# A two-block sequence model on one core: S5's Toeplitz matrices written out whole, one sum per rotation, and a later place for the GLU's splits

## The chip, the core and the metric

The kernel runs on one core of one Trainium2 chip. The metric is the device time of one execution in microseconds, lower is better. Engines are called TensorE (PE in the rows; PEld are its weight loads), VectorE (DVE), ScalarE (ACT), GpSimd (POOL) and SyncE (SP); SP issues every DMA of this program.

## The reference

A model of 256 tokens and 1024 features, all float32. Block one has two layers, each a mixer and a feed-forward with squared ReLU of width 4096, both modulated by a condition vector; the mixer of layer 0 is a gated convolution beside retention, that of layer 1 is S5. A second block follows: gated linear attention, forgetting attention, attention into a memory, gates, and a SwiGLU. The part that the change touches is S5: 64 groups of 16 channels each drive 64 complex states, forward and backward in time,

```
h_t = a h_(t-1) + B u_t          (complex, diagonal a, one system per direction)
y   = Re(C_f h_f) + Re(C_b h_b) + D u
out = (gelu(y) W_a) * sigmoid(gelu(y) W_b)
```

## The kernel before

Activations lie as [128 features, 8 blocks, 256 tokens]. Every dense product runs in three passes of TensorE on weights split in two float32r parts: `piece` (line 309) loads 1 MB of weights by a DMA on SP into one of four buffers (`load`, line 296), and `hilo` (lines 313 to 315) makes of it the high part on ScalarE and the low part on VectorE, a quarter at a time; `lin` (line 323) multiplies. The modulation weights (`ada`, line 429) go through the same four buffers.

**The order of instructions.** The code is traced in order, and a planner then orders each engine's instructions by a simulated time line: on each engine the earliest traced of those that are ready comes first. What is traced as `paced` (line 938) is pinned on TensorE, VectorE and ScalarE behind what was traced last there; SP is not pinned. Each engine then runs its list strictly in order. A tile pool of n buffers makes the writer of a buffer wait for the last reader of the tile that had it.

**S5.** The 256 steps are cut into 32 chunks of 8. Inside a chunk the output is a product with Toeplitz matrices of the kernels at lags -7 to 7; between chunks the states are carried by a scan. All matrices depend on parameters alone. `s5_tables` (line 884) makes them for four groups at a time (i = 0 to 15), a step at a time between the pieces of layer 0's mixer and feed-forward: the matrix from states to outputs V and its write to DRAM (line 897), the kernels by matrix products into one PSUM bank (line 907), their copy by ScalarE into the staging tile Ks, which holds four i and has one buffer (line 911), the matrix from inputs to states W (lines 920 to 922), its transposes by TensorE into the same PSUM bank (line 928), ScalarE's copies (line 929) and their write (line 932). After i = 3, 7, 11 and 15 the four kernels in Ks go to DRAM, each lag once, as rows of 15 lags (lines 916 and 917): eight DMAs.

Layer 1's `s5` (line 956) turns the input into U and Ur by TensorE, then does eight steps (ip), each with two i. `load` (line 1010) reads the tables of a step two steps ahead: W and V in two DMAs each (line 1001), for each pair of steps the Toeplitz matrices Mt by eight DMAs that read overlapping runs of 128 numbers out of the rows of lags (line 1019), and it makes dm, the decay factors of the scan, on GpSimd and ScalarE (lines 1023 and 1024). `chunk_states` makes what each chunk adds to the state (lines 1037 to 1043). `scan` (line 1050) does on VectorE: two products with cosine and sine (1056, 1057), a sum and a difference into PSUM (1058, 1059), the scan (1060), two products back (1064, 1065); then four sums and differences on GpSimd (1067, 1068). `outputs` (line 1071) multiplies by Mt (1079) and V (1081), and for each two steps ScalarE copies the result to Y (1114). `finish` (line 1083) transposes Y, adds D u (1094), applies GELU (1095) and splits the result, for the first half of the steps' channels and at the end for the second. The GLU follows with four pairs of weight pieces; the splits of the first pair are held on VectorE behind the last step's scan:

```
            S = scan(pT.pop(ip), tabs[ip])
            scanned = {mybir.EngineType.DVE: self.last(mybir.EngineType.DVE)}
...
            if j == 0:
                with self.held_at(scanned):
                    Wa, Wb = self.piece("glu_a", j), self.piece("glu_b", j)
```

Of the kernel before, what the change touches and what calls it, by code (L numbers as in the profile page):

```python
# [14 lines left out]
T = 256  # L15
EPS = 1e-6

# columns of the packed per-feature vectors
# [11 lines left out]
def layout(v):  # L30
    """Rearranges the inputs for the DMA engines; no value is changed."""
# [20 lines left out]
    # the same weights with a column to a partition  # L52
# [20 lines left out]
    # S5: group g = 16 e + i, stored in the order (i, e); d = direction  # L73
# [41 lines left out]
class Fill:  # L115
    """Work that is traced a step at a time between the steps of something else."""
# [16 lines left out]
    def settle(self):  # L133
        """Traces the generator that has begun to its end."""
        if self.gens and self.begun is self.gens[0]:
            self.drain(len(self.gens) - 1)

    def drain(self, left=0):
        """Traces all but the last `left` of the generators to their end."""
        while len(self.gens) > left:  # L140
            for _ in self.gens.pop(0):
                pass
        self.credit = 0.0


class Sums:
    """Sums over the features of x^2 w by token, two feature blocks at a time; w(c) [128, m] for block c."""
# [11 lines left out]
    def total(self):  # L159
        """Adds up the squares at hand: one call behind them, so that TensorE need not wait."""  # L160
# [14 lines left out]
class K:  # L175
    def __init__(self, tc, I, out, dbg):
# [4 lines left out]
        self.ntab = {"Wt": 1, "Vt": 1, "Mt": 2, "dm": 2}  # L181
# [37 lines left out]
    def later(self, by):  # L219
        """What is traced here gives way to everything up to `by` instructions further on."""  # L220
# [11 lines left out]
    def last(self, engine):  # L232
        """The name of the last instruction traced on engine."""
        return next(i for i in reversed(list(self.nc.cur_bb.bb.instructions)) if i.engine == engine).name

    def after(self, fill, n, engine, anchor):
        """n steps of fill; on the engine they are issued after the anchor."""
# [8 lines left out]
    def held(self, *engines):  # L246
        """What is traced here is issued behind what was traced last on the engines."""
# [12 lines left out]
    def pinned(self, fill):  # L260
        """The rest of fill, on some engines behind what was traced last."""
# [9 lines left out]
    def behind(self, fill, n=None):  # L271
        """Steps of fill, on DVE behind what was traced last."""
# [10 lines left out]
    # ---- storage  # L283
# [11 lines left out]
    # ---- weights: DMA, split into two float32r parts  # L295
# [27 lines left out]
    def lin(self, ps, W, act, ks, start=True, stop=True, cols=(0, 1)):  # L323
        """ps [128, len(cols), 256] += W[:, k, col block]^T act[:, k']; ks pairs (k of W, k of act)."""
# [6 lines left out]
    def lin_tok(self, ps, W, act):  # L331
        """ps [128 tokens, 2 halves, 256 columns] = act^T W."""
# [24 lines left out]
    def sumsq(self, x, st=None):  # L357
        """[128 tokens, 2 halves, m]: the sums over the features of x^2 w, x [128, 8, T]."""
# [5 lines left out]
    def spread(self, cols, tag=None):  # L364
        """[128, 128 n] in PSUM, on every partition what cols [128, n] holds on partition t in column t of block n."""
# [6 lines left out]
    def rms(self, x, st=None):  # L372
        """The rsqrt of the mean square over the features of x [128, 8, T], on every partition, in PSUM."""
# [3 lines left out]
    def gained(self, x, g):  # L377
        """(hi, lo) of x * g, g [128, 8], and what makes blocks 2 j and 2 j + 1 of them."""
# [12 lines left out]
    def normed(self, x, r, g, shift):  # L391
        """(hi, lo) of x * r * g + shift, g and shift [128, 8]."""
# [13 lines left out]
    # ---- the parts  # L406
    def setup(self):
# [11 lines left out]
        # silu(c), each column 32 times  # L419
# [9 lines left out]
    def ada(self, l, which):  # L429
        """8 of a layer's 48 modulation columns; a generator that yields between pieces."""  # L430
# [18 lines left out]
    def crow(self):  # L449
        """silu(c) along a row, on every partition."""  # L450
# [4 lines left out]
    def ada_v(self, l, which):  # L455
        """The same as ada, on DVE."""
# [16 lines left out]
    def modg(self, l, which, norm):  # L473
        """norm_g * (1 + scale)"""
# [22 lines left out]
    def mixer0(self, x, h, fill, need, after_conv, each):  # L497
# [9 lines left out]
        # gated convolution's input  # L507
# [13 lines left out]
        # what DVE adds up lies in PSUM, where its port is its own  # L521
# [20 lines left out]
        # retention  # L542
# [65 lines left out]
        # layer norm over the 512 channels, silu  # L608
# [79 lines left out]
    # ---- S5: parameters to chunk matrices (chunks of 8 steps), kept in DRAM until they are used  # L688
# [11 lines left out]
    def cmul(self, eng, o, a, b, t):  # L700
        """o = a b for pairs (re, im); t: two scratch tiles."""
# [8 lines left out]
    def exp_exact(self, out, z):  # L710
        """out = e^z, z [128, 64], to float32's accuracy."""
# [14 lines left out]
    def powers(self, PW, u, n, t):  # L726
        """PW[k][:, j] = u^j for j = 0 .. n (n a power of two), pairs (re, im)."""
# [11 lines left out]
    def s5_prep(self):  # L739
# [4 lines left out]
        self.Kd = [dram([16, 16, 240], f"Kd{i}") for i in range(4)]  # L744
# [30 lines left out]
        # powers of a = mag e^(i theta)  # L775
# [6 lines left out]
        # f = (a - 1) / lambda  # L782
# [15 lines left out]
        # what a step's input is worth at its chunk's end, f times a chunk's incoming state at its steps, each with  # L798
        # the sums that make a complex product three real ones
# [19 lines left out]
        # rotation e^(i 8 theta j) and decay |a|^8  # L819
# [21 lines left out]
    def s5_turns(self):  # L841
        """The rotations e^(i 8 theta (j - 16)): those of positive angles, and their mirror images."""
# [19 lines left out]
    def s5_out(self, i):  # L862
        """The matrix from state to outputs of groups 4 i .. 4 i + 3, f C in front: real parts, imaginary ones negated."""
# [11 lines left out]
    def outer(self, eng, out, ab, both, p, i, tag):  # L875
        """For complex a + i b, a and b [128, 4, 16], and powers p, out = (a + b) p0, a p1 and, returned, b p2 of groups 4 i .. 4 i + 3."""
# [7 lines left out]
    def s5_tables(self):  # L884
        """The chunk matrices, four groups at a time."""
        nc, v, work = self.nc, self.nc.vector, self.work
        for i in range(16):
# [7 lines left out]
            # inside a chunk: kernels at lags -7..7  # L895
# [13 lines left out]
            if i % 4 == 0:  # L909
                Ks = work([128, 4, 144], "Ks")  # L910
            nc.scalar.copy(Ks[:, i % 4], pk[:, 0:144])
            if i % 4 == 3:
                Kd = self.Kd[i // 4].rearrange("(i e) c l -> e c i l", e=4)
                for e in range(4):
                    r = 32 * e
                    nc.sync.dma_start(Kd[e, :, :, 112:240], Ks[r:r + 16, :, 0:128])
                    nc.sync.dma_start(Kd[e, :, :, 0:112], Ks[r + 16:r + 32, :, 32:144])
            # inputs to state
# [19 lines left out]
    def paced(self, n):  # L938
        """n steps of the tables, behind what was traced last on three of the engines."""
# [12 lines left out]
    def s5(self, x, u, fill, need, between, each, l=1):  # L952
        """x += gate * GLU(gelu(S5(u))), u [128, ih, s, e, j]: feature block 2 e + ih, step 8 j + s."""
        nc, v = self.nc, self.nc.vector
        # u as [(e, j), i, (s, c)], then [(s, c), i, (e, j)], a chunk's last step first
# [28 lines left out]
        def room(tag, place):  # L984
            """Room for a table of 2048 columns: its own, a weight piece's or that of a piece's parts."""
# [8 lines left out]
        def wide(tag, place, ip):  # L994
            """A table, by group of i."""
# [14 lines left out]
        def load(ip):  # L1010
            Wt = wide("Wt", self.wplace[ip], ip)
            Wt = [w.rearrange("p (e r d q) -> p e r d q", e=4, r=2, d=2) for w in Wt]
            dm = tab([128, 2, 8, 32], "dm")
            if ip % 2 == 0:
                # inside a chunk: the kernels as Toeplitz matrices
                mt.append(room("Mt", self.mplace[ip // 2]).rearrange("p (a i e n) -> p a i e n", a=2, i=2, e=4))
                src = self.Kd[ip // 2]
# [689 lines left out]
```

## Time and profile before

| | |
|---|---|
| device time, three runs | 1226.87, 1230.74 and 1236.1 us, median 1230.74 |
| span of the profiled execution, from its first to its last instruction | 1227.2 us |
| TensorE busy, share of the span | 1169.7 us, 95% |
| VectorE | 891.7 us, 73% |
| ScalarE | 609.7 us, 50% |
| GpSimd | 106.1 us, 9% |
| DMA of the program's own queue | 69864 packets, 265.68 MB, 63.5% of 16 engines' span |

The page gives the span of the profiled execution; what lies around it is not in it, and the runs' times are device times of other executions. The view by stretches gives for each its start and end, its length, then the busy time and count of instructions of PE, PEld, DVE, ACT and POOL, the granted TensorE clock as a share of full speed, the busy share of the DMA engines and what they moved in GB/s. A timeline gives start, duration, engine, line, operation, what is written from what, and in brackets the idle time before and what ended it; equal neighbours are merged (x2). Layer 0's feed-forward lies at about 210 to 434 us, S5 from there to 516 us. A busy TensorE is not one at its peak, since matmuls are pipelined and a lower granted clock makes each longer.

### The profile page before, as it was taken

The page shows a single profiled execution, that of the slowest core. Times are in us where ns is not written, and L with a number is a line of the kernel's source. Part 1 is how long each engine was busy: PE and PEld are TensorE (multiplying, and loading weights), DVE is VectorE, ACT ScalarE, POOL GpSimd, SP SyncE. Part 2 cuts the span into 40 slices and gives each one's busy share as a digit, 9 for nine tenths or more (in the row PEclk, how much of TensorE's full clock was granted, in tenths as well). Part 3 has the DMA queues.
Part 4 walks back from the last instruction along what each step waited for, and adds up shares of the span by engine and source line. Part 5 has one row for each costly group of instructions (what it writes and reads, how often), then busy time and mean ns, then how long its engine had stood idle before and what let it go on. Part 6 is the DMA issues. An engine that isn't in the chain of part 4 may idle for free. (4 is left out here: it accounts for less than half of the span.)

```text
span 1227.2 us, 25417 instructions
## 1 busy us (share of the span) xinstructions
PE 1169.7 (95%) x10482; PEld 1109.3 (90%) x10482; DVE 891.7 (73%) x1821; ACT 609.7 (50%) x1202; POOL 106.1 (9%) x138
## 2 busy tenths in 40 slices
PE   6899897999999976899999999999999999999998
PEld 4698686999999964899999999999999999999998
DVE  7879888889888859767765656686667686665564
ACT  3577244655555542545544545573465545544441
POOL 0077321000000006200000000000000000000000
PEclk8899997999999977799999999999999999999999
DMA  9888886688888999554466655453443454555541
GB/s 341 340 311 327 297 294 212 238 265 282 297 287 267 300 249 309 216 172 171 169 243 212 233 174 172 164 172 104 151 159 138 172 168 148 194 179 177 194 155 60
DMA packets 69979, 267.29 MB, mean 218 GB/s; under 512 B 7380, under 2 KB 35428, under 8 KB 43240
## 3 DMA queue, kind: packets, MB, share of 16 engines
q1 hardware_dynamic: 69864, 265.68, 63.5%
q8 instruction: 82, 1.34, 0.4%
q14 instruction: 33, 0.27, 0.1%
HBM read 246.85 MB, written 18.81 MB: 216 GB/s over the span
## 5 line engine op out<-in xcount | busy, mean ns | idle before, releaser
L315 DVE TENSOR_TENSOR lo<-w,hi 128x512 fp32r<-128x512 f32 (+1 forms) x640 | 427.6, 712 | 147.7 <-ACT hi L314 147.1
L314 ACT ACTIVATE hi<-w 128x512 fp32r<-128x512 f32 (+1 forms) x640 | 358.4, 625 | 337.0 <-PE mm L320 118.8
L319 PE MATMUL mm<-h,hi 128*128 128x256 f32 x1328 | 379.7, 286 | 0.3 <-ACT h L398 0.3
L320 PE MATMUL mm<-h,hi 128*128 128x256 f32 x1328 | 377.7, 285 | 1.3 <-DVE h L399 1.1
L321 PE MATMUL mm<-h,lo 128*128 128x256 f32 x1328 | 378.6, 285 | 0.0
L319 PEld LDWEIGHTS mm<-h,hi 128*128 128x128 f32 x1328 | 254.7, 192 | 7.2 <-issue 3.4
L320 PEld LDWEIGHTS mm<-h,hi 128*128 128x128 f32 x1328 | 254.6, 192 | 2.8 <-DVE h L399 1.5
L321 PEld LDWEIGHTS mm<-h,lo 128*128 128x128 f32 x1328 | 254.5, 192 | 2.6 <-issue 1.6
L321 PE MATMUL at<-s,lo 128*128 128x256 f32 x720 | 204.4, 284 | 1.7 <-DVE lo L315 1.7
L319 PE MATMUL at<-s,hi 128*128 128x256 f32 x720 | 204.8, 284 | 0.0
L320 PE MATMUL at<-s,hi 128*128 128x256 f32 x720 | 204.1, 284 | 0.0
L321 PEld LDWEIGHTS at<-s,lo 128*128 128x128 f32 x720 | 137.9, 192 | 2.5 <-DVE lo L315 2.1
L319 PEld LDWEIGHTS at<-s,hi 128*128 128x128 f32 x720 | 138.0, 192 | 1.8 <-issue 1.4
L320 PEld LDWEIGHTS at<-s,hi 128*128 128x128 f32 x720 | 138.0, 192 | 0.6 <-issue 0.6
L439 PE MATMUL fa<-wa,crep 128*32 128x256 f32 x704 | 56.4, 428 | 7.0 <-DMA wa<-in_ada_dram 3.8
L537 POOL TENSOR_TENSOR s<-s,cv 128x256 f32<-128x256 f32 x60 | 49.9, 866 | 38.9 <-ACT cv L536 38.7
L439 PEld LDWEIGHTS fa<-wa,crep 128*32 128x32 f32 x704 | 23.0, 120 | 27.0 <-issue 6.4
L319 PE MATMUL fp<-h,hi 128*128 128x256 f32 x144 | 41.9, 291 | 0.7 <-ACT h L314 0.7
L320 PE MATMUL fp<-h,hi 128*128 128x256 f32 x144 | 41.8, 290 | 0.0
L321 PE MATMUL fp<-h,lo 128*128 128x256 f32 x144 | 41.6, 289 | 0.0
L929 ACT COPY Wt<-fp 128x512 f32<-128x512 f32 x32 | 18.6, 581 | 43.3 <-PE fp L928 39.9
L536 ACT ACTIVATE cv<-ap,s 128x256 f32<-128x256 f32 x60 | 29.5, 506 | 17.2 <-POOL s L537 16.4
(438 smaller groups left out, 1829.6 us busy)
## 6 DMA issues: line engine op xcount, KB each, us to landing
w<-in_fc_dram SPq DMA_DIRECT2D x64, 1024.0 KB, 5.1
wa<-in_ada_dram SPq DMA_DIRECT2D x44, 1024.0 KB, 6.5
w<-in_w_in_dram SPq DMA_DIRECT2D x38, 1024.0 KB, 4.9
w<-in_w_gate_dram SPq DMA_DIRECT2D x11, 1024.0 KB, 5.0
w<-in_w_up_dram SPq DMA_DIRECT2D x11, 1024.0 KB, 4.9
Vd<-V SPq DMA_DIRECT2D x16, 512.0 KB, 6.6
w<-in_w_out_dram SPq DMA_DIRECT2D x8, 1024.0 KB, 6.2
Wd<-Wt SPq DMA_DIRECT2D x16, 512.0 KB, 5.2
```

The lines of the kernel that those rows point to most:

```text
L314: self.nc.scalar.activation(hi, h, AF.Copy)
L315: self.nc.vector.tensor_tensor(lo, h, hi.bitcast(F32), op=ALU.subtract)
L319: mm(ps, sh, mh, start=start, stop=False, skip_group_check=True)
L320: mm(ps, sh, ml, start=False, stop=False, skip_group_check=True)
L321: mm(ps, sl, mh, start=False, stop=stop, skip_group_check=True)
L439: nc.tensor.matmul(ps[32 * q:32 * q + 32], self.crep[:, 2 * k + k2], w[:, n:n + 256], start=k == 0 and k2 == 0, stop=k == 3 and k2 == 1, t ...
L536: nc.scalar.mul(t, src, w)
L537: nc.gpsimd.tensor_tensor(acc[:, ch], acc[:, ch], t, op=ALU.add)
L929: nc.scalar.copy(W[:, :, k], pt.rearrange("p (e x) -> p e x", e=4))
```

## The change

Kd in DRAM now holds the whole Toeplitz rows, [128 rows (s, c), 4, 8 x 64]: each lag is written to every row that uses it, by 60 DMAs from Ks for each four i, and read back plainly by one DMA of 1 MB. Ks is laid out by lag. The sine factors are made with both signs by ScalarE (sg), so that the two real sums of a rotation become one operation: one on VectorE in place of lines 1058 and 1059, and two on GpSimd in place of four. sg and dm are made after the scan two steps before, no longer in `load`. The splits of the GLU's first weights are held on ScalarE behind the last copy to Y. The pool of small tiles has 10 buffers instead of 12. Comments are dropped.

```diff
-        self.ntab = {"Wt": 1, "Vt": 1, "Mt": 2, "dm": 2}
+        self.ntab = {"Wt": 1, "Vt": 1, "Mt": 2, "dm": 2, "sg": 2}
...
-        self.Kd = [dram([16, 16, 240], f"Kd{i}") for i in range(4)]
+        self.Kd = [dram([128, 4, 8, 64], f"Kd{i}") for i in range(4)]
...
-                Ks = work([128, 4, 144], "Ks")
-            nc.scalar.copy(Ks[:, i % 4], pk[:, 0:144])
+                Ks = work([128, 9, 4, 16], "Ks")
+            nc.scalar.copy(Ks[:, :, i % 4], pk[:, 0:144].rearrange("p (l c) -> p l c", c=16))
             if i % 4 == 3:
-                Kd = self.Kd[i // 4].rearrange("(i e) c l -> e c i l", e=4)
-                for e in range(4):
-                    r = 32 * e
-                    nc.sync.dma_start(Kd[e, :, :, 112:240], Ks[r:r + 16, :, 0:128])
-                    nc.sync.dma_start(Kd[e, :, :, 0:112], Ks[r + 16:r + 32, :, 32:144])
+                Kd = self.Kd[i // 4]
+                for s in range(8):
+                    for e in range(4):
+                        row, r = Kd[16 * s:16 * s + 16, e], 32 * e
+                        nc.sync.dma_start(row[:, 7 - s:8].rearrange("c l n -> c (l n)"), Ks[r:r + 16, 0:s + 1].rearrange("c l i k -> c (l i k)"))
+                        if s < 7:
+                            nc.sync.dma_start(row[:, 0:7 - s].rearrange("c l n -> c (l n)"),
+                                              Ks[r + 16:r + 32, 2 + s:9].rearrange("c l i k -> c (l i k)"))
...
-                src = self.Kd[ip // 2]
-                for s in range(8):
-                    nc.sync.dma_start(mt[-1][16 * s:16 * s + 16].rearrange("c a i e n -> c (a i e) n"),
-                                      bass.AP(tensor=src.tensor, offset=src.offset + 16 * s, ap=[[240, 16], [3840, 16], [1, 128]]))
+                mt.append(room("Mt", self.mplace[ip // 2]).rearrange("p (e l i n) -> p e l i n", e=4, i=4, n=16))
+                nc.sync.dma_start(mt[-1].rearrange("p e l i n -> p (e l i n)"), self.Kd[ip // 2].rearrange("p e l n -> p (e l n)"))
...
+        def factors(ip):
+            Et, rho = self.E[:, :, 8 * ip:8 * ip + 8], self.rho[:, None, 8 * ip:8 * ip + 8, None]
+            sg, dm = tab([128, 2, 8, 32], "sg"), tab([128, 2, 8, 32], "dm")
+            nc.scalar.copy(sg[:, 0], Et[:, 1])
+            nc.scalar.mul(sg[:, 1], Et[:, 1], -1.0)
+            nc.gpsimd.memset(dm[:, :, :, 0], 0.0)
+            nc.scalar.copy(dm[:, :, :, 1:], rho.to_broadcast([128, 2, 8, 31]))
+            return Et[:, 0], sg, dm
...
-            tt(b, pT[:, ::-1, :, 0:31], both(sn[:, :, 1:]), op=ALU.mult)
-            tt(Z[:, 0, :, 1:], a[:, 0], b[:, 0], op=ALU.add)
-            tt(Z[:, 1, :, 1:], a[:, 1], b[:, 1], op=ALU.subtract)
+            tt(b, pT[:, ::-1, :, 0:31], sg[:, :, :, 1:], op=ALU.mult)
+            tt(Z[:, :, :, 1:], a, b, op=ALU.add)
...
-            tt(t[1], Tt[:, ::-1], both(sn), op=ALU.mult)
-            for r, op in ((0, ALU.subtract), (1, ALU.add)):
-                nc.gpsimd.tensor_tensor(S[fw, r], t[0][fw, r], t[1][fw, r], op=op)
-                nc.gpsimd.tensor_tensor(S[bw, r, :, ::-1], t[0][bw, r], t[1][bw, r], op=op)
+            tt(t[1], Tt[:, ::-1], sg[:, ::-1], op=ALU.mult)
+            nc.gpsimd.tensor_tensor(S[fw], t[0][fw], t[1][fw], op=ALU.add)
+            nc.gpsimd.tensor_tensor(S[bw][:, :, :, ::-1], t[0][bw], t[1][bw], op=ALU.add)
...
+        fac = {ip: factors(ip) for ip in range(2)}
...
-            S = scan(pT.pop(ip), tabs[ip])
+            S = scan(pT.pop(ip), fac.pop(ip))
...
+            if ip + 2 < 8:
+                fac[ip + 2] = factors(ip + 2)
             outputs(ip, S, tabs.pop(ip), pY)
             if ip % 2:
                 nc.scalar.copy(Y[:, :, 2 * ip - 2:2 * ip + 2].rearrange("p t i c -> p i t c"), pY.rearrange("p i (t c) -> p i t c", c=16))
+                scanned[mybir.EngineType.Activation] = self.last(mybir.EngineType.Activation)
...
-            self.pools = {t: pool(t, b) for t, b in (("h", 2), ("s2", self.n2), ("q2", self.nq), ("s1", self.n1), ("s0", 12))}
+            self.pools = {t: pool(t, b) for t, b in (("h", 2), ("s2", self.n2), ("q2", self.nq), ("s1", self.n1), ("s0", 10))}
```

## Rows read from the trace of the kernel before

**Rows 1.** view by stretches; start:end, us, then each engine's busy us and instructions

```profile
200.00:430.00 230.00, 228.08 (x2240) 215.02 (x2241) 198.16 (x335) 123.33 (x262) 0.17 (x2) 0.99 0.80 267
...
452.00:496.00 44.00, 32.06 (x628) 23.99 (x624) 39.95 (x60) 11.02 (x21) 22.09 (x35) 0.77 1.04 305
496.00:510.00 14.00, 10.24 (x96) 8.86 (x89) 12.21 (x31) 10.11 (x21) 3.02 (x4) 0.63 0.60 231
```

**Rows 2.** timeline of SP's queue, the bursts; start us, us, engine, line

```profile
234.74 0.33 SPq L916 DMA_DIRECT2D Kd<-Ks  x1
...
239.76 2.52 SPq L298 DMA_DIRECT2D w<-in_fc_dram  x2
...
293.18 0.33 SPq L916 DMA_DIRECT2D Kd<-Ks  x1
...
348.30 0.33 SPq L916 DMA_DIRECT2D Kd<-Ks  x1
...
403.43 0.33 SPq L916 DMA_DIRECT2D Kd<-Ks  x1
...
406.16 0.42 SPq L916 DMA_DIRECT2D Kd<-Ks  x1
```

**Rows 3.** the page's issues and groups, and the view of the tile Ks

```profile
w<-in_fc_dram SPq DMA_DIRECT2D x64, 1024.0 KB, 5.1
...
L314 ACT ACTIVATE hi<-w 128x512 fp32r<-128x512 f32 (+1 forms) x640 | 358.4, 625 | 337.0 <-PE mm L320 118.8
...
L916 SPq DMA_DIRECT2D Kd<-Ks x16: 303/422/733, 234.7 to 406.2; - x16
...
DMA to landing us min/median/max: 1.6/3.6/5.5
```

**Rows 4.** timelines of ScalarE and TensorE in layer 0's feed-forward

```profile
249.41 0.28 ACT L911 COPY Ks<-fp 128x144 f32<-128x144 f32 x1 [1.61 <-issue]
...
254.88 0.60 PE L928 MATMUL fp<-ident,W 128*128 128x128 f32 x4
...
311.01 0.60 PE L928 MATMUL fp<-ident,W 128*128 128x128 f32 x4
...
366.49 0.60 PE L928 MATMUL fp<-ident,W 128*128 128x128 f32 x4
...
427.23 0.28 PE L319 MATMUL at<-s,hi 128*128 128x256 f32 x1
```

**Rows 5.** groups by line and shape, 452 to 510 us: busy, mean, idle

```profile
L1068 POOL TENSOR_TENSOR s<-s,s 64x256 f32<-64x256 f32 x16 | 12.4, 778 | 1.0
...
L1059 DVE TENSOR_TENSOR fa<-q,q 128x248 f32<-128x248 f32 x8 | 6.2, 775 | 0.3
L315 DVE TENSOR_TENSOR lo<-w,hi 128x512 fp32r<-128x512 f32 x8 | 5.8, 788 | 0.0
L1057 DVE TENSOR_TENSOR q<-at,E 128x496 f32<-128x496 f32 x8 | 5.3, 662 | 0.0
...
L1058 DVE TENSOR_TENSOR fa<-q,q 128x248 f32<-128x248 f32 x8 | 3.9, 492 | 0.1
```

**Rows 6.** timeline of S5's loop, VectorE's sums and GpSimd's

```profile
456.45 0.42 DVE L1059 TENSOR_TENSOR fa<-q,q 128x248 f32<-128x248 f32 x1
...
481.22 0.41 DVE L1058 TENSOR_TENSOR fa<-q,q 128x248 f32<-128x248 f32 x1
481.45 0.76 POOL L1067 TENSOR_TENSOR s<-s,s 64x256 f32<-64x256 f32 x1 [1.46 <-DVE s L1065]
...
481.67 0.82 DVE L1059 TENSOR_TENSOR fa<-q,q 128x248 f32<-128x248 f32 x1
```

**Rows 7.** timeline of TensorE, its wait for a Toeplitz read

```profile
490.86 0.65 PE L1079 MATMUL at<-Mt,s 128*32 128x128 f32 x8 [3.21 <-DMA Mt<-Kd]
```

**Rows 8.** timeline of TensorE, end of S5

```profile
500.12 1.08 PE L1081 MATMUL at<-Vt,s 128*32 128x128 f32 x16
...
504.86 0.56 PE L320 MATMUL fp<-h,hi 128*128 128x256 f32 x1
```

More of the change, by code (lines that the diff above doesn't have):

```diff
@@ L1012, in load @@
             Wt = [w.rearrange("p (e r d q) -> p e r d q", e=4, r=2, d=2) for w in Wt]
-            dm = tab([128, 2, 8, 32], "dm")
             if ip % 2 == 0:
-                mt.append(room("Mt", self.mplace[ip // 2]).rearrange("p (a i e n) -> p a i e n", a=2, i=2, e=4))
-                src = self.Kd[ip // 2]
-                for s in range(8):
-                    nc.sync.dma_start(mt[-1][16 * s:16 * s + 16].rearrange("c a i e n -> c (a i e) n"),
-                                      bass.AP(tensor=src.tensor, offset=src.offset + 16 * s, ap=[[240, 16], [3840, 16], [1, 128]]))
-            Mt = mt[-1][:, ip % 2]
-            Et = self.E[:, :, 8 * ip:8 * ip + 8]
-            nc.gpsimd.memset(dm[:, :, :, 0], 0.0)
-            (nc.scalar.copy if self.dm_act else nc.gpsimd.tensor_copy)(dm[:, :, :, 1:], self.rho[:, None, 8 * ip:8 * ip + 8, None].to_broadcast([128, 2, 8, 31]))
+                mt.append(room("Mt", self.mplace[ip // 2]).rearrange("p (e l i n) -> p e l i n", e=4, i=4, n=16))
+                nc.sync.dma_start(mt[-1].rearrange("p e l i n -> p (e l i n)"), self.Kd[ip // 2].rearrange("p e l n -> p (e l n)"))
+            Mt = mt[-1][:, :, :, 2 * (ip % 2):2 * (ip % 2) + 2]
             Vt = wide("Vt", self.vplace[ip], ip)
             Vt = [w.rearrange("p (e r n) -> p e r n", e=4, r=2) for w in Vt]
-            return Wt, Vt, Mt, Et[:, 0], Et[:, 1], dm
+            return Wt, Vt, Mt
+        def factors(ip):
[6 more added lines that the diff above has]
+            return Et[:, 0], sg, dm
         def chunk_states(ip, tabs):
@@ L1048, in s5, with scan @@
         v.memset(Z[:, :, :, 0], 0.0)
-        def scan(pT, tabs):
-            cs, sn, dm = tabs[3:]
+        def scan(pT, fac):
+            cs, sg, dm = fac
             both = lambda a: a[:, None].to_broadcast([128, 2] + list(a.shape[1:]))
@@ L1064, in scan @@
             tt(t[0], Tt, both(cs), op=ALU.mult)
-            tt(t[1], Tt[:, ::-1], both(sn), op=ALU.mult)
-            for r, op in ((0, ALU.subtract), (1, ALU.add)):
-                nc.gpsimd.tensor_tensor(S[fw, r], t[0][fw, r], t[1][fw, r], op=op)
-                nc.gpsimd.tensor_tensor(S[bw, r, :, ::-1], t[0][bw, r], t[1][bw, r], op=op)
+            tt(t[1], Tt[:, ::-1], sg[:, ::-1], op=ALU.mult)
+            nc.gpsimd.tensor_tensor(S[fw], t[0][fw], t[1][fw], op=ALU.add)
+            nc.gpsimd.tensor_tensor(S[bw][:, :, :, ::-1], t[0][bw], t[1][bw], op=ALU.add)
             return S
         def outputs(ip, S, tabs, pY):
-            _, Vt, Mt = tabs[:3]
+            _, Vt, Mt = tabs
             for i in range(2):
@@ L1078, in outputs @@
                         if k == 0:
-                            nc.tensor.matmul(o, U[:, 2 * ip + i, 32 * e:32 * e + 32], Mt[:, i, e], **kw)
+                            nc.tensor.matmul(o, U[:, 2 * ip + i, 32 * e:32 * e + 32], Mt[:, e, :, i], **kw)
                         else:
```

## The prediction

> **What bounds the kernel now.** I read the table of stretches first [rows 1]. In layer 0's feed-forward (200 to 430 us) TensorE is busy 228 of 230 us: whatever holds up TensorE there adds to the time. The S5 stage is the other kind: from 452 to 510 us TensorE is busy only 42 of 58 us, and in the loop, up to 496 us, VectorE is busy 39.95 of 44. So S5 is bound by VectorE's chain, and its DMA engines are full (a share of 1.04) while they move 305 GB/s.
>
> Next I read the SP queue as a timeline [rows 2]. One engine issues every DMA of the program, in order. The reader is to see four bursts of eight Toeplitz writes, starting at 234.74, 293.18, 348.30 and 403.43 us, and what stands behind each: the load of a weight piece follows the first burst at 239.76 us. The seventh issue of the fourth burst starts 2.73 us after its first: 0.455 us an issue.
>
> Then I looked at who needs what stands behind a burst [rows 3, 4], and last at the S5 loop's instructions and its end [rows 5 to 8].
>
> **The change, part by part.**
>
> *Whole rows written.* For each of four tables, 8 x 4 writes of the causal part and 7 x 4 of the other replace 8: 60 issues instead of 8, 240 instead of 32, all on SP under layer 0's feed-forward. The bytes grow from about 1 to 4 MB, which is 3 MB against the 61 MB that 267 GB/s move in 230 us [rows 1]; I cost them at nothing. The issue time I don't. No row shows a write of 16 runs. The upper bound is the row nearest in kind, 0.455 us; the lower is a lone issue's 0.33 us and a few hundredths between two [rows 2]. The rows nearest are the writes of the same tile, 0.42 us each as a median [rows 3]; with a wait between two I take 0.43, near the upper end. A burst then holds SP for 60 x 0.43 = 25.8 us instead of some 4.5.
>
> The Trainium skill, "DMA: Bandwidth & Descriptors", section "Issuing engines are not separate DMA queues", says that the time on the sequencer is usually small relative to the DMA itself. By that the 208 extra issues would cost nothing; the rows show 0.42 us of issue beside 3.6 us to landing, and with sixty in a row the issues are the longer of the two.
>
> Is it hidden? The bursts become ready all at once (the fourth copy into the staging tile Ks readies all 60), and they are traced ahead of the loads of later pieces, so I let SP issue them in one run, as it does the eight. What is queued behind them: weight loads, modulation loads, and table writes. And Ks has one buffer: ScalarE's first copy of the next block (249.41 us in the first case [rows 4]) must wait until all 60 have landed, 3.6 us after the last issue [rows 3]. That copy stands in ScalarE's order ahead of splits of weights, and frees the PSUM bank that TensorE's next table transposes need. These come at 254.88, 311.01 and 366.49 us [rows 4], 18 to 20 us after the bursts begin. With 25.8 us of issue, 3.6 of landing and 0.3 for the copy, they can begin 29.7 us after a burst's start: 264.4, 322.9 and 378.0. TensorE waits 9.6, 11.9 and 11.5 us. The fourth burst has no block behind it; there it is the load behind the burst that counts: issued at 429.2, landed 5.1 us later, its first quarter split in 0.6 + 0.8 [rows 3, 5], so usable at 435.7, and its matmuls stood at 427.23 [rows 4]: 8.5 us. (Behind the other three such loads are late too, but in the same stretch, and I count once.) Sum **+41.5 us**. Bounds: at 0.35 us an issue the same sums give 4.8, 7.1, 6.7 and 3.7, together 22.3; with the bursts as drawn out as the first one was (5.0 us from its start to the next load, 0.63 each [rows 2]) each wait grows by 12, together 89.5. If loads slip in between, 0.
>
> *Plain reads.* 32 reads of 128 KB become 4 of 1 MB. The one wait of TensorE that names such a read is 3.21 us, at 490.86 [rows 7]. It goes; late next are the states from GpSimd, and VectorE is the busy engine there, so it is worth between 0 and 3.2; I take 1.
>
> *One sum per rotation.* On VectorE, lines 1058 and 1059 (8 x 0.492 + 8 x 0.775 = 10.1 us) become eight operations of 128x496; the row of that shape took 0.662 [rows 5]: 5.3. Gain 4.8, all on the path as VectorE bounds the loop. There is a catch: the same 128x248 sum took 0.42 at 456.45 us and 0.82 at 481.67, when GpSimd's sum had begun at 481.45 [rows 6]. GpSimd's sums become twice as long (two of 64x512 for four of 64x256), so a sum caught behind one may wait 1.5 us. If all eight are, each costs 2.2 instead of 1.27, a loss of 7. I take the gain, since line 1058 began at 481.22, ahead of GpSimd's.
>
> The Trainium skill, "SBUF — State Buffer", section "Who interferes with whom", says that an operation of VectorE with two inputs in SBUF and one of GpSimd that reads SBUF block each other for the whole instruction, and that issue order decides. The two durations agree with it. By the worse issue order at every step, the sum would be that loss of 7.
>
> GpSimd's four sums cost some 4 x 0.778 = 3.1 us a step [rows 5]; two of twice the size cost between half of that and all of it; only the last step's is on the path, I take 0.3 gained. ScalarE gets two operations of 128x256 more a step for the sines of both signs, between 0.28 (128x144 [rows 4]) and 0.6 us each: some 16 x 0.4 = 6.4 us, hidden, as it is busy 11 of 44 us [rows 1]. Each waits for VectorE's last reading of the old factors, and the copy of the next chunk states stands behind it; GpSimd's 3 us hide that. Without that cover the 6.4 us would be on the path.
>
> *GLU's splits behind S5's last copy.* Queued behind are eight splits on ScalarE and, through them, eight on VectorE of 0.788 us [rows 5]. Today TensorE's outputs end with the 16 that start at 500.12, and its unbroken GLU work starts at 504.86 [rows 8]: 3.7 us later. With the hold, copy, split and subtraction (0.6 + 0.6 + 0.8) could let it start 2.0 us behind, a gain of 1.7; or VectorE's 6.3 us of subtractions come too late, a loss of up to 5.8. I take 0.
>
> S5 together: -1 - 4.8 - 0.3 = **-6.1 us**, between -10.0 and about +13.
>
> Smaller room (10 small buffers instead of 12) and the removed comments: 0.
>
> Sum: 41.5 - 6.1 = +35.4. On the profiled execution's span of 1227.2 us that is 1262.6; the median of the three runs shown stands 3.5 us above that span, and I carry it: **1266 us**.
>
> **The rivals.**
>
> *The copies cost nothing.* Loads overtake, or an issue with 16 runs is far cheaper than any row. For it: nothing in the trace shows sixty in a row. Against it: after the first burst the load of the next piece was issued right behind the eight, at 239.76, and no issue of such writes took under 0.30 us [rows 2, 3]. Then S5's -6.1 stands alone: 1227.2 - 6.1 + 3.5 = 1224.6. The sentence of the skill's DMA page above stands for this case.
>
> *S5's stage gives much more, and the issues are hidden: faster.* Its DMA engines are full and slow [rows 1], and reads in short runs may hold back the loop's other tables. Then the whole 3.2 us of the wait, the 4.8, the 0.3 and the 1.7 at the end go, 10.0, and TensorE's clock, 0.63 of full speed in the 14 us from 496 [rows 1], gives up to 0.37 x 14 = 5 more: 1227.2 - 15 + 3.5 = 1216. It decides only if the bursts cost under 2.7 us together, which needs SP free again before a burst's 18 us of lead are used up, at an issue under 0.24 us.
>
> *Worse than forecast.* Issues as drawn out as in the first burst, and the port against the sum: 1227.2 + 89.5 + 13 + 3.5 = 1333 at most; half of that excess, about 1300, is what I would still expect to see.
>
> *The change doesn't do what it says:* the planner draws the writes apart or orders ScalarE's copy later. Half the forecast's cost: 1227.2 + 20.7 - 6.1 + 3.5 = 1245.
>
> **How the numbers follow.** The forecast 0.47 (1248 to 1288, from the bounds of the issue and of S5), the drawn-apart form 0.12, worse 0.05, copies for nothing 0.20, faster 0.16. About 1% (12 us: below 1218.4, above 1243.0) is what a measurement of this kernel tells from no change. Faster: 0.16 and a tenth of the free case, 0.18. Slower: 0.47 + 0.05 and half of the drawn-apart form, 0.58. The same: 0.24. Range: 1212 to 1288 leaves out the worse case and the lower part of the faster one. The forecast's own range is 1248 to 1288.
>
> **What would show it.** Right: 60 Toeplitz writes in one run on SP per block, 0.4 us apart; behind them a ScalarE copy into Ks that waits for a DMA; TensorE idle 8 to 12 us four times between 250 and 440 us, with a lower clock behind; S5's loop some 0.6 us a step shorter; no wait on the Toeplitz reads. Wrong: TensorE still busy to 99% in the feed-forward, loads between the writes, or issues of 0.2 us.

## The result, and the profile after

The changed kernel is slower: 1283.8 us median (1279.56 to 1287.05), against 1231.59 us for the kernel before, run beside it (1226.87 to 1236.1), a ratio of 1.0426 [1.04, 1.0451]. The profiled execution's span is 1285.3 us, 58.1 more than before's 1227.2. That is 5.9 us more than the 52.2 between the medians: the profiled execution after is the longest of its four runs, and before's span is short beside its runs' median. The forecast was 1266 with a range of 1212 to 1288: the case and its mechanism came about, at a larger size, 4 us inside the upper end of a wide range.

Where the time lies is read first from the start times of three instructions that both kernels have (taken from the timelines, us from the span's start):

| kernel, profiled execution | last residual sum of layer 0's feed-forward (L483) | first chunk product of S5 | first sum of the GLU | end |
|---|---|---|---|---|
| before | 435.37 | 451.82 | 525.66 | 1227.2 |
| after | 487.73 | 506.69 | 579.86 | 1285.3 |

The feed-forward ends 52.4 us later. The way to S5's first product takes 18.96 us for 16.45; S5 itself, from there to the GLU's first sum, 73.17 for 73.84; all behind that 705.4 for 701.5. The last difference is not put down to the change: the version below with two Ks buffers runs the same code there in 702.3, and the thirteen profiled kernels of this case take between 701.5 and 705.5. The 6.1 us that the change was to gain in S5 have not come.

The view by stretches of the kernel after; columns as in [rows 1], which they answer. The first row is the feed-forward from 200 us on, the next three the ends of the first three bursts, the last two S5's loop and its end:

```profile
200.00:490.00 290.00, 252.15 (x2296) 233.07 (x2294) 200.45 (x336) 126.98 (x263) 0.00 (x0) 0.88 0.59 202
...
262.00:280.00 18.00, 8.25 (x57) 6.58 (x58) 8.57 (x16) 5.32 (x13) 0.00 (x0) 0.55 0.80 280
...
340.00:360.00 20.00, 13.49 (x91) 10.48 (x92) 12.39 (x20) 6.79 (x15) 0.00 (x0) 0.52 0.98 341
...
412.00:440.00 28.00, 18.32 (x132) 15.31 (x133) 15.53 (x26) 10.70 (x22) 0.00 (x0) 0.63 0.93 330
...
507.00:551.00 44.00, 27.08 (x589) 21.65 (x580) 34.68 (x48) 14.82 (x31) 17.34 (x19) 0.88 1.03 412
551.00:565.00 14.00, 9.23 (x125) 8.00 (x126) 11.57 (x29) 8.80 (x17) 4.70 (x4) 0.77 0.42 146
```

And the same stretch of the kernel before, cut where its feed-forward ends:

```profile
200.00:436.00 236.00, 233.80 (x2288) 220.65 (x2288) 199.91 (x339) 124.01 (x264) 0.17 (x2) 0.99 0.81 266
```

The two hold about the same TensorE instructions (2296 and 2288). TensorE stands idle for 290 - 252.15 = 37.9 us where it stood for 2.2: 35.7 us of stalls. It is also busy 18.4 us longer with the same work, while the granted clock is 0.88 instead of 0.99. Together 54.0 us, of which 1.6 lie behind the last residual sum, where the two windows do not end equally far: this is the whole 52.4 of the feed-forward. And VectorE is busy 34.68 of 44 us in the loop, where it was the bound with 39.95 [rows 1]: it now waits.

SP's queue in the timeline of the kernel after, the first burst and what stands behind it (answers to [rows 2]):

```profile
235.24 0.34 SPq L918 DMA_DIRECT2D Kd<-Ks  x1
235.63 0.41 SPq L920 DMA_DIRECT2D Kd<-Ks  x1
...
263.83 1.85 SPq L918 DMA_DIRECT2D Kd<-Ks  x4
265.79 0.37 SPq L936 DMA_DIRECT2D Wd<-Wt  x1
266.25 1.47 SPq L897 DMA_DIRECT2D Vd<-V  x2
267.77 1.43 SPq L859 DMA_DIRECT2D bc<-in_bc_dram  x1
269.26 2.38 SPq L298 DMA_DIRECT2D w<-in_fc_dram  x3
```

Sixty writes in one run, 235.24 to about 265.3; behind them three table writes, a read of parameters, and at 269.26 the first load of a weight piece since 227.0 us. The other bursts begin at 309.90, 383.78 and 458.92; the four last 30.0, 29.5, 30.2 and 32.4 us to their last issue. The view of the tile Ks in the same kernel (duration in ns as least/median/most, start of first and last; answers to [rows 3]):

```profile
L918 SPq DMA_DIRECT2D Kd<-Ks x128: 302/418/1660, 235.2 to 491.3; - x128
L920 SPq DMA_DIRECT2D Kd<-Ks x112: 302/418/1822, 235.6 to 489.5; - x112
...
DMA to landing us min/median/max: 1.4/1.6/5.9
```

An issue takes 418 ns as a median, the start of the next follows 463 ns after its own, and the write has landed 1.6 us later: the run of issues is the long part, not the transfer.

Who waits, in ScalarE's and TensorE's timelines after (answers to [rows 4]; in brackets the idle time ahead of the instruction and what ended it):

```profile
267.04 0.28 ACT L911 COPY Ks<-fp 128x144 f32<-128x144 f32 x1 [6.25 <-DMA Kd<-Ks]
267.37 1.12 PE L932 MATMUL fp<-ident,W 128*128 128x128 f32 x4 [7.60 <-ACT Ks L911]
269.32 1.12 PE L932 MATMUL fp<-ident,W 128*128 128x128 f32 x4 [0.83 <-ACT Wt L933]
271.11 2.00 PE L907 MATMUL fp<-V,tiny 128*32 128x16 f32 x32 [0.68 <-ACT Wt L933]
274.62 1.09 PE L932 MATMUL fp<-ident,W 128*128 128x128 f32 x4 [1.52 <-DVE W L926]
277.07 0.58 PE L319 MATMUL at<-s,hi 128*128 128x256 f32 x1 [1.36 <-ACT hi L314]
...
341.46 1.12 PE L932 MATMUL fp<-ident,W 128*128 128x128 f32 x4 [7.91 <-ACT Ks L911]
...
416.31 1.11 PE L932 MATMUL fp<-ident,W 128*128 128x128 f32 x4 [5.28 <-ACT Ks L911]
```

This is the forecast's chain link by link: ScalarE's first copy of the next block waits for the burst to land, and the transposes wait for the copy, 7.60, 7.91 and 5.28 us. Four or five smaller waits follow each time, 14.8 us in all. The transposes themselves take 1.12 us where they took 0.60 [rows 4]: in that stretch (262 to 280 us) the granted clock is 0.55 of full speed, near the lower of its two levels, 1.2 of 2.4 GHz.

### The profile page after: what moved, and what is told of

Its sections match the earlier page's. It is cut to its first block, busy times and chain, and to the rows that moved or that the text cites. A ratio compares the mean times of both kernels' runs of the same rounds, so it can differ in the third digit from the quotient of the medians.

```text
span 1285.3 us, 25552 instructions
## 1 busy us (share of the span) xinstructions
PE 1183.9 (92%) x10482; PEld 1120.7 (87%) x10482; DVE 889.3 (69%) x1813; ACT 617.3 (48%) x1218; POOL 103.1 (8%) x122
## 5 line engine op out<-in xcount | busy, mean ns | idle before, releaser
L319 PE MATMUL at<-s,hi 128*128 128x256 f32 x720 | 208.2, 289 | 3.6 <-ACT hi L314 3.6
L320 PE MATMUL at<-s,hi 128*128 128x256 f32 x720 | 207.2, 288 | 0.0
L319 PEld LDWEIGHTS at<-s,hi 128*128 128x128 f32 x720 | 141.4, 196 | 6.6 <-ACT hi L314 6.2
L321 PEld LDWEIGHTS at<-s,lo 128*128 128x128 f32 x720 | 140.8, 196 | 1.7 <-DVE lo L315 1.5
L320 PEld LDWEIGHTS at<-s,hi 128*128 128x128 f32 x720 | 141.4, 196 | 0.4 <-issue 0.4
L932 PE MATMUL fp<-ident,W 128*128 128x128 f32 x128 | 24.7, 327 | 29.3 <-ACT Ks L911 20.8
L439 PEld LDWEIGHTS fa<-wa,crep 128*32 128x32 f32 x704 | 21.8, 120 | 31.5 <-DMA wa<-in_ada_dram 9.8
L932 PEld LDWEIGHTS fp<-ident,W 128*128 128x128 f32 x128 | 17.6, 166 | 33.2 <-ACT Ks L911 21.7
```

The source lines that it names most:

```text
L319: mm(ps, sh, mh, start=start, stop=False, skip_group_check=True)
L320: mm(ps, sh, ml, start=False, stop=False, skip_group_check=True)
L321: mm(ps, sl, mh, start=False, stop=stop, skip_group_check=True)
L439: nc.tensor.matmul(ps[32 * q:32 * q + 32], self.crep[:, 2 * k + k2], w[:, n:n + 256], start=k == 0 and k2 == 0, stop=k == 3 and k2 == 1, t ...
L932: nc.tensor.transpose(pt[:, 128 * e:128 * e + 128], Wn[:, k, e].rearrange("p s c -> p (s c)"), self.ident)
```

## Experiments

Medians and ratios are against the kernel before, run beside them (1231.72, 1231.84 and 1231.09 us in the three sets).

**The whole rows alone.** The kernel before with only the row writes, the new layout of Ks and Kd and the plain reads:

```diff
+                for s in range(8):
+                    for e in range(4):
+                        row, r = Kd[16 * s:16 * s + 16, e], 32 * e
...
+                nc.sync.dma_start(mt[-1].rearrange("p e l i n -> p (e l i n)"), self.Kd[ip // 2].rearrange("p e l n -> p (e l n)"))
```

> The kernel before with the whole Toeplitz rows written and read plainly, and nothing else of the change. Theory (SP's queue): sixty issues of 0.46 us in one run, four times, starve TensorE of weights in layer 0's feed-forward, which was 53 us longer in the changed kernel; so 1280 to 1290 us, and the first-to-last residual of that feed-forward again some 52 us late. Rival (the other parts carry much of the loss): 1240 to 1265 us.

1286.82 us, ratio 1.0453 [1.0436, 1.047]. The rows carry the whole loss.

**All but the whole rows.** Sums, sines, GLU hold and the 10 small buffers, with the eight writes and eight reads of before.

```diff
-                        row, r = Kd[16 * s:16 * s + 16, e], 32 * e
...
+                    nc.sync.dma_start(Kd[e, :, :, 112:240], Ks[r:r + 16, :, 0:128])
+                    nc.sync.dma_start(Kd[e, :, :, 0:112], Ks[r + 16:r + 32, :, 32:144])
```

> The changed kernel with the old rows of lags, written by eight DMAs and read by eight. Theory: the one sum per rotation and the later GLU splits are a small gain when SP is free, 1222 to 1229 us against 1231.6 before, S5's scans some 0.5 us closer to each other. Rival (the port: a sum caught behind a GpSimd sum twice as long; GLU splits too late): 1232 to 1243 us.

1231.42 us, ratio 0.9996 [0.9986, 1.0006]: no gain, between the two expectations. In the profiled execution S5 does get shorter, 71.0 us from the first chunk product to the GLU's first sum for 73.84, but all behind that takes 703.8 for 701.5, so the medians alone decide. What takes back part of S5's gain stands in TensorE's timeline, and what follows from it in VectorE's:

```profile
493.04 0.66 PE L1082 MATMUL at<-Mt,s 128*32 128x128 f32 x8 [5.10 <-DMA m<-in_mem_dram]
```

```profile
470.89 1.63 DVE L1063 TENSOR_TENSOR fa<-q,q 128x496 f32<-128x496 f32 x1
...
477.04 0.67 DVE L1063 TENSOR_TENSOR fa<-q,q 128x496 f32<-128x496 f32 x1
...
497.08 0.69 DVE L1069 TENSOR_TENSOR s<-fp,sg 128x512 f32<-128x512 f32 x1 [3.81 <-PE at L1084]
```

The last scan starts at 491.24 instead of 492.31, but the last Toeplitz matrix is only there at 493.04 (490.86 before [rows 7]; the row's releaser is the DMA that follows the eight reads on SP), and VectorE then waits 3.81 us for TensorE. The sum takes 0.67 us, and 1.63 where GpSimd's is in its way.

**Two Ks buffers** in the kernel after:

```diff
-        bufs = {"V": 2, "bc": 3}.get(tag, 1)
+        bufs = {"V": 2, "bc": 3, "Ks": 2}.get(tag, 1)
```

> The changed kernel with two buffers for the staging tile Ks, so that ScalarE's copy of the next block need not wait until the sixty writes have landed. Theory (SP's queue): the loads behind the burst are late all the same, so only the surplus of the Ks wait over the load's delay goes: 1268 to 1282 us. Rival (the single buffer Ks is the cause): 1228 to 1245 us.

1280.3 us, ratio 1.0393 [1.0371, 1.0415]. No copy into Ks waits for a row write any more, and yet at most some 3.5 us come back (the two intervals overlap). TensorE's transposes now wait for the copies of W's transposes, and those for the table writes to DRAM, which stand on SP behind the burst; view of waits, 200 to 490 us (us in total, times, longest):

```profile
ACT Wt L933 <- DMA Wd<-Wt: 25.6, 8, 7.8
...
PE fp L932 <- ACT Wt L933: 23.9, 3, 9.5
```

The buffer was only the first of the burst's victims.

**Issues without bytes.** The kernel before and 52 writes of 16 x 64 bytes behind each eight, into memory that nothing reads:

```diff
+            if i % 4 == 3:
+                for m in range(52):
+                    r = 32 * (m % 4)
+                    nc.sync.dma_start(self.Xd[i // 4][:, m], Ks[r:r + 16, m % 3, 0:16])
```

> The kernel before with 52 further DMAs behind the eight writes of each block, each of 16 x 64 bytes from Ks to a scratch tensor: sixty issues in a row as in the changed kernel, but 0.05 MB a block more instead of 0.8. Theory (the issues): layer 0's feed-forward is 45 to 55 us longer again, 1272 to 1290 us in all. Rival (the bytes and runs of the larger writes load the DMA engines): 1232 to 1240 us.

1273.01 us, ratio 1.0333 [1.0319, 1.0347]: 41.3 us for 208 issues of 1 KB each, with the same median of 418 ns. Not bytes, then. But they did not stand in one run behind the eight. Each reads one of the first three copies into Ks (`m % 3`), so a third of them was ready behind each of these copies, ahead of the eight, and they went out among the loads, in runs of up to 17 and at most 18 between two weight loads, 8.4 us of issue: by the forecast's own rule, which compares a run with 18 us of lead, they should have cost little. Setting SP's issues beside the landings gives a reading of part of it. SP's DMAs land on eight semaphores in turn, and from 200 to 500 us no DMA of SP starts before the eighth DMA ahead of it, which has the same semaphore, has landed, in this kernel and in those before and after. Here 63.9 of the 110.0 us of gaps between SP's issues in the feed-forward end within 0.15 us of that landing (41 gaps); in the kernel before 9.0 of 180.3, in the kernel after 5.4 of 122.8. Read so, a write of 1 KB takes one of eight places that 1 MB loads and table writes then lack; no run tests it by itself. ScalarE's longest waits are again for table writes, view of waits, us in total, times, longest:

```profile
ACT Wt L934 <- DMA Wd<-Wt: 50.6, 9, 9.4
```

**Twenty-two** of them instead of 52:

> The kernel before, with 22 extra writes of 16 x 64 bytes behind each four i's eight Toeplitz writes (into memory that nothing reads), so a block has 30 issues instead of 8. The 52-write version took 1273.0, 41.3 us more than before. Theory A (a burst costs only what exceeds its lead, 18 us from its start to TensorE's next table work): 30 x 0.465 = 14 us fits inside the lead, so 1231 to 1238. Rival B (each issue on SP costs the same share, since SP's whole time in the feed-forward is what runs short): 22/52 x 41.3 = 17.5, so 1246 to 1252.

1235.2 us, ratio 1.0026 [1.0015, 1.0038]. Not proportional: 22 extra issues a block cost 3.4 us, 52 cost 41.3. They too stood among the loads, at most 8 between two, so the time falls where the lead theory had it without testing a run of 30. In the profiled execution the feed-forward is not late at all (its last residual at 434.25 us); the loss is in S5, where one scan starts 9.16 us after the one before it instead of 4.87, as TensorE waits 5.8 us for a read of W's tables. Why that read is late no view here shows.

**GpSimd issues the rows.** The kernel after with two Ks buffers and another queue:

```diff
-                        nc.sync.dma_start(row[:, 7 - s:8].rearrange("c l n -> c (l n)"), Ks[r:r + 16, 0:s + 1].rearrange("c l i k -> c (l i k)"))
+                        nc.gpsimd.dma_start(row[:, 7 - s:8].rearrange("c l n -> c (l n)"), Ks[r:r + 16, 0:s + 1].rearrange("c l i k -> c (l i k)"))
...
```

> The kernel after, with two Ks buffers and the 240 row writes issued by GpSimd instead of SP (GpSimd is busy 0.2 of 230 us in layer 0's feed-forward); the same bytes, sources and destinations. Theory A (the cost is SP's place ahead of the loads): the feed-forward returns to its time of before, 435 us for its last residual, and the whole to 1222 to 1236, since the plain reads and the single sums are then free of their price. Rival B (the writes themselves, 16 runs each, slow the other transfers whoever issues them): 1268 to 1284.

1229.73 us, ratio 0.9984 [0.9972, 0.9996]. The same 240 writes, the same bytes, and 50.6 us are gone against the two-buffer version. The timeline of GpSimd in this kernel, its first burst:

```profile
236.68 0.67 POOL L918 DMA_DIRECT2D Kd<-Ks  x1 [38.87 <-ACT Ks L911]
237.34 0.49 POOL L920 DMA_DIRECT2D Kd<-Ks  x1
...
242.09 0.48 POOL L918 DMA_DIRECT2D Kd<-Ks  x1 [1.40 <-DMA Kd<-Ks]
...
278.87 0.48 POOL L918 DMA_DIRECT2D Kd<-Ks  x1 [1.45 <-DMA Kd<-Ks]
```

And the feed-forward by stretches:

```profile
200.00:437.00 237.00, 234.18 (x2291) 220.78 (x2289) 200.83 (x346) 123.55 (x262) 99.52 (x208) 0.99 0.83 282
```

The burst even takes longer, 42 us, and TensorE is busy 234 of 237 us at a clock of 0.99. What cost the time was that SP issued them, ahead of loads and table writes. (GpSimd's DMAs also land on eight semaphores of their own, so SP's loads have all of theirs; this run takes away issue time and shared places together.)

**The rows handed out by sixes.** Two Ks buffers, the 60 writes traced three pairs at a time (rows) between the steps of the next tables:

```diff
+                todo = [(Kd, Ks, s, e) for s in range(8) for e in range(4)]
...
+            rows(3)
...
```

> The kernel after, with two Ks buffers and the 60 row writes of a block handed out six at a time between the steps of the next tables' work instead of in one go; the same 240 issues, the same bytes. Theory A (the single run of 60 is what delays the loads and table writes behind it): no load is late by more than 6 x 0.463 = 2.8 us, the stalls go, 1228 to 1242. Rival B (SP's total time of 240 x 0.463 = 111 us is what counts, wherever it lies): about as the version with two Ks buffers alone, 1268 to 1284.

1288.42 us, ratio 1.0465 [1.0448, 1.0482], above both expectations. The edit did not do what it was for: SP is not pinned, the writes were ready, and the planner put them ahead of the loads, with 60, 54, 60 and 60 of them between one weight load and the next. It separates nothing except where code is traced and where it is issued.

**The rows given way.** The same, by priority:

```diff
+                        with self.later(60 * (4 * s + e)):
...
```

> The kernel after with two Ks buffers, the same 240 row writes on SP, each pair of them given a later priority than the pair before it, so that in SP's order other work goes between: at most 20 writes stand between two weight loads in the first three blocks (60, 54, 60 and 60 in the handed-out version that took 1288.4), and 60 stand together only at the end of the fourth. Theory A (what counts is how many writes stand ahead of a load that is waited for): 20 x 0.463 = 9.3 us fit inside the 18 us of lead, only the last run can cost, 1232 to 1248. Rival B (SP's total time in the feed-forward, 111 us more than before, is what counts): 1265 to 1285.

1256.97 us, ratio 1.0204 [1.0188, 1.0221]: neither theory. The same issues and bytes on the same queue cost 31.5 us less than handed out, so the order counts. But 25.9 us stay, 24.6 of them in the feed-forward (last residual at 459.97 us), with at most 20 writes between two loads in the first three blocks; so a run's length against the lead isn't the whole here either. Of the 95.5 us of gaps on SP in the feed-forward 31.2 end with the landing of the eighth DMA ahead. And the view of waits names the table writes again:

```profile
ACT Wt L934 <- DMA Wd<-Wt: 26.5, 5, 7.7
```

How the 24.6 us divide between SP's issue time and its eight places is open: no run here gave SP more places.

**Rows laid out from DRAM to DRAM.** The version without whole rows, and behind the eight writes eight copies of 128 KB, each making 16 of the whole rows out of the rows of lags; S5 reads them plainly:

```diff
+                for s in range(8):
+                    nc.sync.dma_start(self.Md[i // 4][16 * s:16 * s + 16],
+                                      bass.AP(tensor=src.tensor, offset=src.offset + 16 * s, ap=[[240, 16], [3840, 16], [1, 128]]))
```

> The single sums, both-sign sines and the GLU hold as in the version without whole rows (1231.4), the eight lag writes of before, and behind them 8 copies from DRAM to DRAM a block that lay the Toeplitz rows out under layer 0's feed-forward, so that S5 reads each 1 MB plainly. Theory A (in the version without whole rows the Toeplitz read took back the sums' gain: TensorE waits 5.10 us for its last one at 493.04, where before waited 3.21 us): with plain reads that wait goes and the gain of 3 to 5 us shows; 16 issues a block, 7.4 us, fit inside the 18 us of lead: 1225.5 to 1229.5. Rival B (another transfer or GpSimd's states take its place): 1230 to 1232.

1227.28 us, ratio 0.9963 [0.995, 0.9975]: the gain shows once the reads are plain. Two more complete the square. The copies and plain reads without the sums:

> The kernel before with only the 8 copies from DRAM to DRAM a block and the plain reads of 1 MB; sums, sines and GLU order as before. The version with these and the single sums took 1227.3, the sums without plain reads 1231.4, before 1231.8. Theory A (each alone only moves the wait: reads come early but VectorE's chain of 4.87 us a step stays, sums shorten the chain but the last read is late): 1230 to 1232.5, so that the gain appears only with both. Rival B (the plain reads carry the gain by themselves, since the 3.21 us wait for the last one goes): 1226.5 to 1229.

1229.72 us, ratio 0.9982 [0.9971, 0.9993], between the theories. Sums alone give 0.9996, reads alone 0.9982, both 0.9963: somewhat more than the two added, though the intervals do not settle by how much. And the last version without the GLU hold:

> The version that took 1227.3 (single sums, copies from DRAM to DRAM, plain reads) without the hold of the GLU's first splits on ScalarE. Theory A (the hold is worth nothing either way, as predicted): 1226 to 1228.5. Rival B (without it the splits stand ahead of S5's last copy and delay the GLU's first products by 1.7 us): 1228.5 to 1230.5. Rival C (the hold makes VectorE's splits late, so that going without it gains): 1222 to 1225.5.

1226.65 us, ratio 0.9964 [0.9951, 0.9977]: the hold is worth nothing. These two are the fastest versions, 0.4% below the kernel before; the copies alone and the rows on GpSimd's queue lie 0.2% below it, with intervals that just exclude 1.

## Why the prediction was right, and what it missed

**Right: the rows cost, and how.** With the rows alone the kernel is as slow as with the whole change (1.0453 beside 1.0426). In the kernel after it is one run of 60 per block; a ScalarE copy behind it that waits for a DMA; TensorE's transposes behind the copy. The transposes were forecast 29.7 us after a burst's start and came 32.1, 31.6 and 32.5 us after. The pitch was 0.463 us for 0.43, and a few gaps made bursts of 30 us for 25.8; the landing, 1.6 us for 3.6, gave 2 of that back. The gaps could be seen before: from first to last issue the four bursts of eight took 3.5 to 5.4 us, 0.50 to 0.77 an issue, and the 0.43 left them out. But the copy into Ks is not the one link that counts: with a second buffer the same bursts stop TensorE by way of the table writes, at about the same price. The Trainium skill, "DMA: Bandwidth & Descriptors", section "Issuing engines are not separate DMA queues", which the prediction weighed, says that issuing from several engines only saves sequencer time, usually small beside the DMA. For sixty such writes in a row it was not small here: 418 ns an issue beside 1.6 us to landing, and 50.6 us between the two queues.

**Mis-sized: the term of +41.5 us.** It measured 52.4, and its parts were not those summed, so that the forecast came as near as it did is in part luck; and a range from 1212 to 1288, which holds no change as well, says little by being met. The three waits on the copy were 7.60 + 7.91 + 5.28 = 20.8 us for a forecast 33.0, because TensorE reached its transposes only 24.5, 23.6 and 27.2 us after the burst's start and not 18 to 20. The smaller waits behind them, 14.8, make up the rest of the 35.7 us of stalls. And 18.4 us more of busy time go with the lower clock in the wake of the stalls, which the prediction named as a sign and gave no price.

**Wrong place: the fourth burst.** 8.5 us were forecast for the last weight load of the feed-forward. The fourth burst came at 458.92 to 491.35, ran past the feed-forward's end at 487.73 and had no weight load of it behind, but a table write and all of S5's first reads. SP's, ScalarE's and TensorE's timelines after:

```profile
491.86 0.37 SPq L936 DMA_DIRECT2D Wd<-Wt  x1
...
494.89 0.60 ACT L1033 COPY dm<-rho 128x496 f32<-128x496 f32 x1 [3.82 <-DMA Wd<-Wt]
...
499.25 1.12 PE L965 MATMUL at<-ident,s 128*128 128x128 f32 x4 [5.94 <-ACT s L1160]
```

ScalarE's first decay factors wait for the last table write, issued at 491.86 behind the burst; TensorE's first transposes of S5's input wait for ScalarE. So the loop starts 2.5 us late (and 1.7 late in the version whose rows GpSimd issues, where no burst stands on SP). In the loop itself the eight scans span 39.2 us, and 33.0 in that version, with the same code. No view shows late tables there: from 507 to 551 us TensorE's queues wait 0.3 us in all for a read. VectorE waits 8.0 us for TensorE's transposes of the chunk states, and these for ScalarE, in whose order the copy of the chunk states stands behind that of the decay factors, which waits for VectorE's scan. One step of it, timelines of VectorE, ScalarE and TensorE after:

```profile
528.03 1.23 DVE L1066 TENSOR_TENSOR_SCAN fp<-dm,fa 128x512 f32<-128x512 f32 x1
529.37 0.60 ACT L1033 COPY dm<-rho 128x496 f32<-128x496 f32 x1 [3.47 <-DVE fp L1066]
529.88 0.58 ACT L1046 COPY s<-mm 128x512 f32<-128x512 f32 x1
530.51 0.66 PE L1050 MATMUL at<-ident,s 128*128 128x128 f32 x4 [2.00 <-ACT s L1046]
```

The transposes for the next step begin when this step's scan is over. In the version with copies from DRAM, at the same step, they begin while it runs, since the copy stands ahead in ScalarE's order:

```profile
472.97 0.59 ACT L1046 COPY s<-mm 128x512 f32<-128x512 f32 x1 [1.97 <-POOL s L1073]
473.51 1.23 DVE L1066 TENSOR_TENSOR_SCAN fp<-dm,fa 128x512 f32<-128x512 f32 x1
474.22 0.65 PE L1050 MATMUL at<-ident,s 128*128 128x128 f32 x4
```

The next scan comes 5.95 us later in the one (533.98) and 4.48 in the other (477.99). Both orders are the planner's, of the same code; why it chose otherwise in the kernel after and in the one with two Ks buffers is not shown. The rows handed out by sixes, on SP too, have the shorter loop (33.3 us).

**S5's -6.1 us** did not come in the kernel after (-0.7 from the first chunk product to the GLU's first sum), and yet their sum was about right. Freed of the burst, that stretch takes 68.5 us (GpSimd's queue), 69.3 (copies from DRAM) and 67.6 (without the hold) for 73.84: -4.5 to -6.2 (the medians of these three gain less on the kernel before, 2.1 to 4.6 us). In the kernel after, a premise failed: ScalarE's work on the factors was to be hidden, and the step above has it on the path. The rows weigh on S5 too: alone, without any of the other parts, they stretch it to 79.0 us, and the kernel after has 5.8 us less than that. The parts were mis-sized both ways, and that they cancel is luck. The plain reads alone (with the copies) shorten this stretch by 3.7 us, to 70.2, where 1 was taken of the 3.2 us of the wait; the sums and the hold without them by 2.8, to 71.0, for 5.1. And where the reads are plain, the sums bring the first and the last scan 2.5 us closer together, 32.9 us for 35.4, not 4.2 (seven steps of 0.6). Where some of the 4.8 us of the sums went shows in the last version's timelines of GpSimd, VectorE and ScalarE:

```profile
472.23 1.27 POOL L1073 TENSOR_TENSOR s<-s,s 64x512 f32<-64x512 f32 x1
472.72 1.32 DVE L1065 TENSOR_TENSOR fa<-q,q 128x496 f32<-128x496 f32 x1
473.53 0.59 ACT L1046 COPY s<-mm 128x512 f32<-128x512 f32 x1 [1.98 <-POOL s L1073]
```

A sum that starts behind GpSimd's takes 1.32 us instead of 0.67, and ScalarE's copy of the chunk states, which TensorE and then VectorE need for the next step, waits for GpSimd's as well; by the code it writes a buffer of the pool that GpSimd's operands come from. The catch of [rows 6] hits some steps, not all, one of eight here and two in the kernel after: the eight sums average 763 ns in the version with copies and 868 in the kernel after, against 0.66 forecast. This agrees with the Trainium skill, "SBUF — State Buffer", section "Who interferes with whom", as the prediction read it. The GLU hold at 0: 1227.28 us with it and 1226.65 without.

**The rivals.** That copies cost nothing fell. The faster one, with 1216, would not have come even without the burst: the best versions gain 4.4 and 4.6 us, not 15. The writes were not drawn apart in the kernel after.

## What to carry to other kernels

Count the DMAs that a change adds on the one queue that also loads the weights, and multiply by the measured pitch before counting bytes; then see what stands behind them there and how many may be under way, and move them to an idle engine's queue or make fewer of them. Here TensorE's stalls cost their own length and half as much again in busy time at a lower clock behind them (35.7 and 18.4 us). And a shorter chain gains only if what it will meet earlier is early too: the last read (5.10 us of wait in the version without whole rows), and the other engines' places in their orders.

## What was not expected of the hardware

An issue of 1 KB costs SP as much as one of up to 32 KB: 418 ns as a median in every version that has such writes. GpSimd's queue issues the same writes at 484 ns, little slower, with waits for earlier writes between groups of eight. From 200 to 500 us in these kernels SP never had more than eight DMAs under way, large or small: the ninth waited for the first to land. The trace shows this as eight semaphores taken in turn; whether another program could have more under way, no run here shows. And 22 extra issues a block cost 3.4 us where 52 cost 41.3: by these two points the queue has slack up to some number of issues; where it ends is not measured.
